# Sliding-window attention: the two halves of a unit's probabilities are added into one square before they are transposed

## The chip, the cores and the metric

The kernel runs on one core of a Trainium2 chip. The metric is the device time of one execution in microseconds (us). The whole network of four layers is one program; the change concerns two of the four layers.

## The reference, cut to what matters

The model is a stack of four layers over 16 learned tokens and 1024 input tokens of width 1024: attention, mLSTM, HGRN2, attention. The change lies in the attention layers (`i % 3 == 0`, that is layers 0 and 3). There a block of 128 queries sees its own block of 128 keys and the one before, within a window of 128:

```python
dist = (jnp.arange(BLOCK)[:, None] + BLOCK) - jnp.arange(2 * BLOCK)[None, :]
band = (dist >= 0) & (dist < A_WIN)          # BLOCK = A_WIN = 128
s = jnp.where(mask, einsum(q, kk) * A_HD ** -0.5, -jnp.inf)
m = jnp.maximum(s.max(axis=-1), sink)
e = jnp.exp(s - m[..., None])
p = e / (e.sum(axis=-1) + jnp.exp(sink - m))[..., None]
o = jnp.einsum('bnhgqk,bnkhd->bnqhgd', p, vv)
```

For query i of a block the band keeps key j (0 to 255, the block before first) where j > i and j <= i + 128. So of the keys j and j + 128 exactly one is inside the window of each query: where the left half of a row of `p` is not zero the right half is zero, and the reverse. This is what the change uses.

## The kernel before

Each layer projects its input on TensorE (PE) with float32 operands split into a high and a low part, so that each product is three matmuls (L231 for the tiles of weights, L281, L326 for the output projection). PE's order is written out: a list of steps, each with a cost in nanoseconds, in which two lists are merged in proportion to their costs by `weave`. The order on VectorE (DVE), ScalarE (ACT), GpSimd (POOL) and the DMA queue (SP) is set by a scheduler that follows data dependencies and priorities.

The attention itself is cut into units. A unit is one block `b` of queries (9 blocks of which block 0 has the 16 learned tokens), one `pair` of tiles of heads (4 pairs) and one half `hh` of those tiles; it handles two heads, index `u`. Layer 0 has 72 units and layer 3 has 64, since it leaves out block 0. The units of a pair run one after the other, with block as the outer and `hh` as the inner loop. While one pair is attended, PE also gets the projections for later pairs ("fill"), and these differ by pair: little of it beside pairs 0 and 3, more beside pairs 1 and 2. A unit has three steps, two units apart on PE: at the turn of unit k, PE gets V_step of unit k-4, T_step of unit k-2, S_step of unit k.

- **S_step** (L701): four matmuls make the scores `S` [128, 2, 256] in PSUM (L726, L727). A custom DVE operation (L734, one per head) adds the mask, scales, and leaves the scores and their row minimum in the SBUF tile `Sm`; ACT takes the exponential in place with the row's sum (L737, one per head); DVE takes the reciprocal (L739); POOL multiplies the 2 x 256 probabilities by it (L740). POOL also writes the sink's column of `Sm` ahead of that (L731). `Sm` has two buffers, so units k and k+2 share one.
- **T_step** (L743): PE transposes `Sm` in four pieces of 128 x 128 (two halves, two heads, L755) into one PSUM tile `pt`. ACT copies `pt` to `Ph`, the part of higher value (L757), and DVE subtracts it from `pt` to make `Pl` (L758).
- **V_step** (L760): four matmuls with `Ph` and `Pl` (L773) add up the output `po`, which ACT and DVE move to the rows `o` (L781, L782).

The mask tile `masks` is read by L734 at its columns 128 to 383; its entry is 0 inside the window and 1e30 outside, because L734 works with the sign reversed and takes a minimum.

Of the kernel before, what the change touches and what calls it, by code (L numbers as in the profile page):

```python
# [9 lines left out]
F32 = mybir.dt.float32  # L10
F32R = mybir.dt.float32r
AF = mybir.ActivationFunctionType
ALU = mybir.AluOpType
PSUM = bass.MemoryType.PSUM

P = 128
# [97 lines left out]
def hybrid_kernel(ctx: ExitStack, tc: tile.TileContext, ins, out, layers=(0, 1, 2, 3)):  # L114
    nc = tc.nc
    v, s, g, pe, sp = nc.vector, nc.scalar, nc.gpsimd, nc.tensor, nc.sync
# [11 lines left out]
    def nm(x):  # L128
        ctr[0] += 1
        return f"{x}{ctr[0]}"  # L130
# [16 lines left out]
    def psum(tag, bufs):  # L147
        return ps.tile([P, 512], F32, tag="p", name=nm(tag), bufs=8)
# [331 lines left out]
    def layer_a(i, j, first, last, fin, scale=None):  # L480
# [3 lines left out]

        def enter():
            R["mix"] = mix = new_mix()
            R["masks"] = masks = mix.tile([P, 384], F32, name=nm("masks"))
            sp.dma_start(masks, ins["a_masks"])
            R["cons"] = cons = mix.tile([P, 18], F32, name=nm("cons"))
            sp.dma_start(cons, ins["a_cols"][j])  # L490
            v.tensor_scalar(cons[:, 0:1], cons[:, 0:1], -0.125, None, op0=ALU.mult)
            v.tensor_scalar(cons[:, 2:18], cons[:, 2:18], -1.0, None, op0=ALU.mult)
# [205 lines left out]
        def mixers():  # L698


            def S_step(w):  # L701
                mix, cons = R["mix"], R["cons"]
                b, hh, n = w["b"], w["hh"], w["n"]
                kh, kl = R["k", w["pair"] // 2][hh]
                q0, nq = blk(b)
                qb = slice(q0 - chunks[n][0], q0 - chunks[n][0] + nq)
                kq = CHUNK_BLOCKS[n].index(b)
                if b == 0:
                    k0, kbs = 0, ((0, 0, 16),)
                elif b == 1:  # L710
                    k0, kbs = 0, ((0, 0, 16), (1, 16, 128))
                else:
                    k0, kbs = q0 - P, ((b - 1, 0, 128), (b, 128, 128))
                w["kbs"] = kbs
                nk = sum(z[2] for z in kbs)
                kw, mo = (nk if b == 0 else 256), {0: 128, 1: 112}.get(b, 0)
                kb = slice(k0, k0 + kw)
                S = psum("pm", 2).rearrange("p (u k) -> p u k", u=2)
                w["Sm"] = Sm = mix.tile([P, 2, 257], F32, tag="Sm", name=nm("Sm"), bufs=2)
                if b == 0:  # L720
                    g.memset(Sm[:, :, :NMETA], 0.0)
                st, den = small(2), small(2)
                sinks = []
                for u, t in enumerate(w["ts"]):
                    q = R["q", t, n][hh]
                    pe.matmul(S[:nq, u, :kw], q[:, qb], kh[:, kb], start=True, stop=False)  # L726
                    pe.matmul(S[:nq, u, :kw], q[:, qb], kl[:, kb], start=False, stop=True)  # L727
                    head = (2 * (t // 4) + hh) * 4 + t % 4
                    sinks.append(cons[:nq, 2 + head : 3 + head])
                    if u == 0:  # L730
                        g.tensor_copy(Sm[:nq, :, nk : nk + 1], cons[:nq, 2 + head : 4 + head].rearrange("p (u c) -> p u c", c=1))  # L731
                for u in range(2):
                    rq = R["rq", w["ts"][u], n][:nq, 2 * kq + hh : 2 * kq + hh + 1]
                    v.tensor_tensor_reduce(Sm[:nq, u, :nk], S[:nq, u, :nk], R["masks"][:nq, P + mo : P + mo + nk],  # L734
                                           rq, sinks[u], ALU.add, ALU.min, st[:nq, u : u + 1])
                for u in range(2):
                    s.activation(Sm[:nq, u, : nk + 1], Sm[:nq, u, : nk + 1], AF.Exp, scale=-1.0,  # L737
                                 bias=st[:nq, u : u + 1], accum_out=den[:nq, u : u + 1])
                v.reciprocal(den[:nq], den[:nq])  # L739
                g.tensor_tensor(Sm[:nq, :, :nk], Sm[:nq, :, :nk],  # L740
                                den[:nq].rearrange("p (u c) -> p u c", c=1).to_broadcast([nq, 2, nk]), op=ALU.mult)

            def T_step(w):  # L743
                b, kbs, Sm = w["b"], w["kbs"], w["Sm"]
                nq = blk(b)[1]
                kn = NMETA if b == 0 else P
                pt = psum("pt", 1).rearrange("p (k u q) -> p k u q", k=2, u=2)
                w["Ph"] = Ph = R["mix"].tile([P, 2, 2, P], F32R, tag="Ph", name=nm("Ph"), bufs=2)
                w["Pl"] = Pl = R["mix"].tile([P, 2, 2, P], F32R, tag="Pl", name=nm("Pl"), bufs=2)
                if b == 0:  # L750
                    for z in (Ph, Pl):
                        g.memset(z[:, 0, :, :NMETA].bitcast(F32), 0.0)
                for ki, (kb, ko, _) in enumerate(kbs):
                    for u in range(2):
                        pe.transpose(pt[:kn, ki, u, :], Sm[:, u, ko : ko + kn], ident)  # L755
# [800 lines left out]
def _layout(inp):  # L1556
# [1 line left out]
    meta, xx = np.asarray(inp["meta"]), np.asarray(inp["x"])[0]  # L1558
    f["xT"] = np.concatenate([meta, xx], axis=0).T.reshape(KT, P, T)
    f["ngain"] = np.asarray(inp["norm_gain"]).reshape(4, KT, P).transpose(2, 0, 1)  # L1560
    am = np.zeros((P, 384), np.float32)
    am[:64, :64] = 1.0
    am[64:, 64:128] = 1.0
    ii = np.arange(P)[:, None]
    jj = np.arange(256)[None]
    am[:, 128:] = np.where((jj > ii) & (jj <= ii + P), 0.0, -BIG)
    f["a_masks"] = am
    f["b_mask"] = np.where(ii <= np.arange(P)[None], 0.0, BIG).astype(np.float32)
# [76 lines left out]
```

## Time and profile before

| what | value |
|---|---|
| time of three runs, median (lowest to highest) | 2595.86 us (2591.49 to 2597.38) |
| the profiled execution: its time, its span | 2594.76 us, 2593.0 us |
| granted TensorE clock, mean | 0.997 |
| PE busy | 2547.2 us (98%) |
| DVE, ACT, POOL busy | 1949.5 us (75%), 1682.9 us (65%), 243.4 us (9%) |
| units of attention with `b > 1` | 56 in each of the two layers, 112 in all |

The share of an engine is its busy time over the span of all four layers; attention takes about the first 415 us and the stretch from about 2200 to 2530 us. A row of a group of instructions names the line of the kernel, the engine, the operation, what is written and read, the shapes and the count; then busy us and mean ns of one; then how long the engine was idle just before and what ended that. A row of the timeline begins with the start in us from the start of the span and the duration.

### The profile page before, as it was taken

The page shows a single profiled execution, that of the slowest core. Times are in us where ns is not written, and L with a number is a line of the kernel's source. Part 1 is how long each engine was busy: PE and PEld are TensorE (multiplying, and loading weights), DVE is VectorE, ACT ScalarE, POOL GpSimd, SP SyncE. Part 2 cuts the span into 40 slices and gives each one's busy share as a digit, 9 for nine tenths or more (in the row PEclk, how much of TensorE's full clock was granted, in tenths as well). Part 3 has the DMA queues.
Part 4 walks back from the last instruction along what each step waited for, and adds up shares of the span by engine and source line. Part 5 has one row for each costly group of instructions (what it writes and reads, how often), then busy time and mean ns, then how long its engine had stood idle before and what let it go on. Part 6 is the DMA issues. An engine that isn't in the chain of part 4 may idle for free.

```text
span 2593.0 us, 54342 instructions
## 1 busy us (share of the span) xinstructions
PE 2547.2 (98%) x20446; PEld 2487.2 (96%) x20446; DVE 1949.5 (75%) x5266; ACT 1682.9 (65%) x4403; POOL 243.4 (9%) x564
## 2 busy tenths in 40 slices
PE   8999999999999999999999999999999999999999
PEld 8899999999999999999999999999999999999999
DVE  7897898785657474747475688978878978887996
ACT  8766766576464555555555757877676857767772
POOL 0321231000000000000000000001000000321330
PEclk9999999999999999999999999999999999999999
DMA  5223212021111111111111111111111113212112
GB/s 157 62 66 95 57 43 70 29 67 54 46 50 49 51 41 58 42 50 45 53 42 50 58 35 34 35 35 35 34 42 34 35 51 93 64 43 82 56 42 78
DMA packets 86058, 140.21 MB, mean 54 GB/s; under 512 B 12425, under 2 KB 39186, under 8 KB 85794
## 3 DMA queue, kind: packets, MB, share of 16 engines
q1 hardware_dynamic: 85794, 136.73, 17.1%
q8 instruction: 161, 2.64, 0.4%
q14 instruction: 103, 0.84, 0.1%
HBM read 121.83 MB, written 4.27 MB: 49 GB/s over the span
## 4 chain that ended last, share of the span: by engine, by line
PE 62%; DVE 13%; ACT 8%; issue 2%; DMA 1%; SPq 0%; POOL 0%; DVEq 0%; ACTq 0%; POOLq 0%
PE pj L231 28%; PE pj L326 14%; PE pj L281 10%; DVE wl L196 1%; PE po L1019 1%; PE po L1021 1%; PE pa L1035 1%; ACT X L1269 1%; PE po L773 1%; DVE x L329 1%; PE pj L277 1%; ACT Sm L737 1%; PE pt L755 1%; DVE Sm L734 1%; DVE X L1267 1%
## 5 line engine op out<-in xcount | busy, mean ns | idle before, releaser
L231 PE MATMUL pj<-uh,wh 128*128 128x256 f32 (+2 forms) x2688 | 915.7, 341 | 7.7 <-ACT uh L401 7.2
L231 PE MATMUL pj<-ul,wh 128*128 128x256 f32 (+2 forms) x2688 | 864.3, 322 | 0.3
L231 PE MATMUL pj<-uh,wl 128*128 128x256 f32 (+2 forms) x2688 | 864.6, 322 | 0.0
L231 PEld LDWEIGHTS pj<-uh,wh 128*128 128x128 f32 x2688 | 508.5, 189 | 17.4 <-ACT uh L401 7.2
L231 PEld LDWEIGHTS pj<-ul,wh 128*128 128x128 f32 x2688 | 508.8, 189 | 6.4 <-DVE ul L196 0.8
L231 PEld LDWEIGHTS pj<-uh,wl 128*128 128x128 f32 x2688 | 507.9, 189 | 0.0
L196 DVE TENSOR_TENSOR wl<-wr,wh 128x512 fp32r<-128x512 f32 (+1 forms) x338 | 234.2, 703 | 55.0 <-ACT wh L195 52.1
L195 ACT CAST wh<-wr 128x512 fp32r<-128x512 f32 (+1 forms) x338 | 202.7, 613 | 97.6 <-PE pj L326 31.5
L326 PE MATMUL pj<-yh,wh 128*128 128x384 f32 (+2 forms) x768 | 253.6, 330 | 9.8 <-DVE x L329 8.3
L329 DVE TENSOR_TENSOR x<-x,pj 128x384 f32<-128x384 f32 (+2 forms) x480 | 233.8, 507 | 33.4 <-PE pj L326 32.1
L326 PE MATMUL pj<-yh,wl 128*128 128x384 f32 (+2 forms) x768 | 246.2, 321 | 0.0
L326 PE MATMUL pj<-yl,wh 128*128 128x384 f32 (+2 forms) x768 | 246.2, 321 | 0.0
L281 PE MATMUL pj<-wh,uh 128*128 128x256 f32 (+1 forms) x768 | 232.7, 303 | 0.0
L281 PE MATMUL pj<-wl,uh 128*128 128x256 f32 (+1 forms) x768 | 216.3, 282 | 0.0
L281 PE MATMUL pj<-wh,ul 128*128 128x256 f32 (+1 forms) x768 | 215.9, 281 | 0.0
L737 ACT ACTIVATE Sm<-Sm,s 128x257 f32<-128x257 f32 (+2 forms) x272 | 131.1, 483 | 88.6 <-DVE s L734 86.3
L740 POOL TENSOR_TENSOR Sm<-Sm,s 128x512 f32<-128x512 f32 (+2 forms) x136 | 139.3, 1024 | 406.5 <-DVE s L739 386.3
L458 ACT ACTIVATE t<-t 128x384 f32<-128x384 f32 (+2 forms) x240 | 118.0, 491 | 75.5 <-DVE t L457 74.6
L195 ACT CAST yh<-r 128x384 fp32r<-128x384 f32 (+2 forms) x120 | 57.0, 478 | 156.2 <-PE pj L326 139.4
L326 PEld LDWEIGHTS pj<-yh,wh 128*128 128x128 f32 x768 | 144.9, 189 | 14.0 <-DVE x L329 10.3
L457 DVE SCALAR_TENSOR_TENSOR t<-pj,t 128x400 f32<-128x400 f32 (+2 forms) x168 | 86.3, 513 | 81.5 <-ACT t L456 80.2
L281 PEld LDWEIGHTS pj<-wh,uh 128*128 128x128 f32 x768 | 144.7, 188 | 2.2
(303 smaller groups left out, 5447.1 us busy)
## 6 DMA issues: line engine op xcount, KB each, us to landing
wr<-in_b_win SPq DMA_DIRECT2D x124, 256.0 KB, 2.8
wr<-in_a_win SPq DMA_DIRECT2D x80, 256.0 KB, 2.8
wr<-in_c_win SPq DMA_DIRECT2D x64, 256.0 KB, 3.0
wr<-in_a_wout SPq DMA_DIRECT2D x32, 256.0 KB, 2.8
wr<-in_b_wout SPq DMA_DIRECT2D x32, 256.0 KB, 2.7
t<-t SPq DMA_DIRECT2D x100, 48.0 KB, 1.9
cs<-in_rope SPq DMA_DIRECT2D x11, 400.0 KB, 3.7
cs<-in_rope SPq DMA_DIRECT2D x11, 384.0 KB, 3.5
```

Of the source, the lines that this page charges most:

```text
L195: s.copy(h, src)
L196: v.tensor_tensor(l, src, h.bitcast(F32), op=ALU.subtract)
L231: pe.matmul(acc[:, :cn], a[:, k, :], b[:, k, c0 : c0 + cn], start=(k == 0 and i == 0), stop=(k == KT - 1 and i == 2))
L277: pe.matmul(acc[:48, :nc], um[0][:, k, :], m[:, kk, :], start=(k == 0 and m is wh), stop=(k == KT - 1 and m is wl))
L281: pe.matmul(acc[:cn, :nc], a[:, k, c0 : c0 + cn], m[:, kk, :], start=(k == 0 and j == 0), stop=(k == KT - 1 and j == 2))
L326: pe.matmul(acc[:, :cn], a[:, k, mc], b, start=(k == 0 and i == 0), stop=(k == 1 and i == 2))
L329: v.tensor_tensor(x[:, m, c0 : c0 + cn], x[:, m, c0 : c0 + cn], acc[:, :cn], op=ALU.add)
L457: v.scalar_tensor_tensor(a[:, :cn], z, 0.0, a[:, :cn], op0=ALU.min, op1=ALU.subtract)
L458: s.activation(a[:, :cn], a[:, :cn], AF.Exp)
L734: v.tensor_tensor_reduce(Sm[:nq, u, :nk], S[:nq, u, :nk], R["masks"][:nq, P + mo : P + mo + nk], rq, sinks[u], ALU.add, ALU.min, st[:nq, u ...
L737: s.activation(Sm[:nq, u, : nk + 1], Sm[:nq, u, : nk + 1], AF.Exp, scale=-1.0, bias=st[:nq, u : u + 1], accum_out=den[:nq, u : u + 1])
L740: g.tensor_tensor(Sm[:nq, :, :nk], Sm[:nq, :, :nk], den[:nq].rearrange("p (u c) -> p u c", c=1).to_broadcast([nq, 2, nk]), op=ALU.mult)
```

## The change

For the units with `b > 1`, POOL first adds the right half of `Sm` to the left (L742 of the new kernel), so that a square of 128 x 128 per head holds all 128 keys of each query's window. The multiplication by the reciprocal (L743) then covers 2 x 128 elements instead of 2 x 256, and PE makes two transpositions instead of four (L758). A DVE operation takes the minimum of each transposed square with a mask of 1e30 or 0, once for either half, and writes the 2 x 2 x 128 results back to the buffer of `Sm` (L762). ACT copies from there to `Ph` (L763), and the subtraction that makes `Pl` moves from DVE to POOL (L764). The mask is a window of one more column in `masks`, which grows from 384 to 385 columns. Blocks 0 and 1 are as before.

```diff
                 v.reciprocal(den[:nq], den[:nq])
+                if b > 1:
+                    nk = P
+                    g.tensor_tensor(Sm[:, :, :P], Sm[:, :, :P], Sm[:, :, P : 2 * P], op=ALU.add)
                 g.tensor_tensor(Sm[:nq, :, :nk], Sm[:nq, :, :nk],
                                 den[:nq].rearrange("p (u c) -> p u c", c=1).to_broadcast([nq, 2, nk]), op=ALU.mult)
...
-                pt = psum("pt", 1).rearrange("p (k u q) -> p k u q", k=2, u=2)
+                pt = psum("pt", 1)
...
+                if b > 1:
+                    for u in range(2):
+                        pe.transpose(pt[:, P * u : P * u + P], Sm[:, u, :P], ident)
+                    src = Sm.rearrange("p u k -> p (u k)")[:, :512].rearrange("p (k u q) -> p k u q", k=2, u=2)
+                    both = pt[:, : 2 * P].rearrange("p (k u q) -> p k u q", k=1, u=2)
+                    keep = R["masks"][:, P + 1 : 3 * P + 1].rearrange("p (k u q) -> p k u q", k=2, u=1)
+                    v.tensor_tensor(src, both.to_broadcast([P, 2, 2, P]), keep.to_broadcast([P, 2, 2, P]), op=ALU.min)
+                    s.copy(Ph, src)
+                    g.tensor_tensor(Pl, src, Ph.bitcast(F32), op=ALU.subtract)
+                    return
+                pt = pt.rearrange("p (k u q) -> p k u q", k=2, u=2)
...
-    jj = np.arange(256)[None]
+    jj = np.arange(257)[None]
```

On PE the order of the steps is the same before and after; only the run of four transpositions of a unit becomes a run of two. The queues of the other engines are laid anew by the scheduler. GpSimd's queue in pair 0 of layer 0, before, for units 11, 12 and 13 (`Sm_1359`, `Sm_1407`, `Sm_1454` are their tiles of probabilities, `cons` holds the sinks, `s` the reciprocal):

```order
L731 COPY Sm_1359<-cons_188 128x2
L740 TENSOR_TENSOR Sm_1303<-Sm_1303,s_1305 128x2x256
L731 COPY Sm_1407<-cons_188 128x2
L740 TENSOR_TENSOR Sm_1359<-Sm_1359,s_1361 128x2x256
L731 COPY Sm_1454<-cons_188 128x2
L740 TENSOR_TENSOR Sm_1407<-Sm_1407,s_1409 128x2x256
```

The same place after, where the tiles of the three units are `Sm_1360`, `Sm_1408` and `Sm_1455`, and `Pl_1401`, `Pl_1442` are the results of the subtraction for units 10 and 11:

```order
L742 TENSOR_TENSOR Sm_1360<-Sm_1360 128x2x128
L743 TENSOR_TENSOR Sm_1360<-Sm_1360,s_1362 128x2x128
L764 TENSOR_TENSOR Pl_1401<-Sm_1304,Ph_1400 128x512
L731 COPY Sm_1408<-cons_188 128x2
L742 TENSOR_TENSOR Sm_1408<-Sm_1408 128x2x128
L743 TENSOR_TENSOR Sm_1408<-Sm_1408,s_1410 128x2x128
L764 TENSOR_TENSOR Pl_1442<-Sm_1360,Ph_1441 128x512
L731 COPY Sm_1455<-cons_188 128x2
```

One multiplication per unit has become an addition, a multiplication and a subtraction, and the subtraction for a unit stands behind the multiplication of the next unit. Of the 112 units, 100 have this order; in 12 the subtraction stands ahead of that multiplication.

VectorE's queue at the same place, before (unit 12; `pm` are its scores):

```order
L734 ISA Sm_1407,s_1408<-pm_1406,masks_186,cons_188,rq_570 128x256
L734 ISA s_1408 128x1
L758 TENSOR_TENSOR Pl_1399<-pt_1397,Ph_1398 128x512
L734 ISA Sm_1407,s_1408<-pm_1406,masks_186,cons_188,rq_634 128x256
L734 ISA s_1408 128x1
L528 TENSOR_TENSOR qs_1475<-t_1239,qs_1475 64x400
L782 TENSOR_TENSOR r_977<-r_977,po_1323 64x256
L739 RECIPROCAL s_1409<-s_1409 128x2
```

And after, from unit 12's scores to those of unit 13:

```order
L734 ISA Sm_1408,s_1409<-pm_1407,masks_186,cons_188,rq_570 128x256
L734 ISA s_1409 128x1
L734 ISA Sm_1408,s_1409<-pm_1407,masks_186,cons_188,rq_634 128x256
L734 ISA s_1409 128x1
L762 TENSOR_TENSOR Sm_1360<-pt_1440,masks_186 128x512
L796 TENSOR_TENSOR r_977<-r_977,po_1325 64x256
L739 RECIPROCAL s_1410<-s_1410 128x2
L528 TENSOR_TENSOR qs_1477<-t_1241,qs_1477 64x400
L528 TENSOR_TENSOR qs_1480<-t_1241,qs_1480 64x400
L796 TENSOR_TENSOR r_978<-r_978,po_1325 64x256
L734 ISA Sm_1455,s_1456<-pm_1454,masks_186,cons_188,rq_570 128x256
```

The minimum for unit 11 (L762) stands behind the scores of unit 12 and ahead of its reciprocal, and the first operation on unit 13's scores writes into the buffer that unit 11 has had, so it waits for the subtraction `Pl_1442` on GpSimd.

More of the change, by code (lines that the diff above doesn't have):

```diff
@@ L486, in enter @@
             R["mix"] = mix = new_mix()
-            R["masks"] = masks = mix.tile([P, 384], F32, name=nm("masks"))
+            R["masks"] = masks = mix.tile([P, 385], F32, name=nm("masks"))
             sp.dma_start(masks, ins["a_masks"])
```

2 lines of the change are left out of this document (1 added, 1 removed).

## The prediction

> **What bounds the kernel now.** I read the page first: how busy the engines are, and the chain that ended last.
>
> ```profile
> PE 2547.2 (98%) x20446; PEld 2487.2 (96%) x20446; DVE 1949.5 (75%) x5266; ACT 1682.9 (65%) x4403; POOL 243.4 (9%) x564
> PE 62%; DVE 13%; ACT 8%; issue 2%; DMA 1%; SPq 0%; POOL 0%; DVEq 0%; ACTq 0%; POOLq 0%
> ```
>
> PE is busy nearly all the time and holds most of the chain. GpSimd is on it with 0%. So a transposition saved looks like time saved, and work on GpSimd looks free. Those are averages over four layers, so next I look at the attention alone: how far apart are the units? Each unit has four transpositions, so their first and last start in a stretch, and their count, give the period. First four stretches beside pairs 0 and 3, then two of pair 1, then two of pair 2:
>
> ```profile
> L755 PE MATMUL pt<-ident,Sm x48: 270/272/330, 82.3 to 121.5; 128*128 128x128 f32 x48
> L755 PE MATMUL pt<-ident,Sm x44: 270/272/328, 361.2 to 397.3; 128*128 128x128 f32 x44
> L755 PE MATMUL pt<-ident,Sm x48: 270/272/328, 2212.7 to 2251.0; 128*128 128x128 f32 x48
> L755 PE MATMUL pt<-ident,Sm x48: 270/272/275, 2476.0 to 2517.2; 128*128 128x128 f32 x48
> L755 PE MATMUL pt<-ident,Sm x48: 270/272/299, 155.5 to 217.3; 128*128 128x128 f32 x48
> L755 PE MATMUL pt<-ident,Sm x48: 270/272/273, 2277.8 to 2342.9; 128*128 128x128 f32 x48
> L755 PE MATMUL pt<-ident,Sm x56: 270/272/306, 279.4 to 341.6; 128*128 128x128 f32 x56
> L755 PE MATMUL pt<-ident,Sm x56: 270/272/300, 2399.1 to 2462.7; 128*128 128x128 f32 x56
> ```
>
> Less 0.3 us for the last unit's own four, the first four rows are 11, 10, 11 and 11 periods in 38.9, 35.8, 38.0 and 40.9 us: 43 periods of 3.57 us on average, the quick stretches. Pair 1 has 5.6 and 5.9 us, pair 2 has 4.8 and 4.9 us. So PE gives the other engines 3.57 us per unit at the least. What do they do with it? Two of the quick stretches by windows (busy us of PE, PEld, DVE, ACT, POOL), and who PE waited for in all of the program:
>
> ```profile
> 361.10:396.90 35.80, 34.99 (x248) 34.19 (x247) 32.65 (x87) 27.14 (x76) 13.96 (x20) 1.00 0.20 58
> 2212.70:2250.60 37.90, 37.90 (x286) 37.58 (x284) 32.79 (x96) 30.54 (x94) 14.98 (x23) 1.00 0.17 49
> PE pt L755 <- POOL Sm L740: 10.0, 9, 2.2
> PEld pt L755 <- POOL Sm L740: 12.9, 12, 2.5
> ```
>
> PE is full there, but VectorE is at 91% and 87%, GpSimd at 39%. And of the few waits that PE has in attention, the one that comes back is for GpSimd's multiplication (22.9 us in 21 times). Attention is close to a second bound, the way from scores to transposition.
>
> **The change: what PE saves.** The timeline shows the four transpositions of a unit as one piece, and the groups give the mean of one:
>
> ```profile
> 200.36 0.60 PE L755 MATMUL pt<-ident,Sm 128*128 128x128 f32 x4
> L755 PE MATMUL pt<-ident,Sm 128*128 128x128 f32 x512 | 77.4, 274 | 8.3 <-POOL Sm L740 7.8 <-DVE s L734 0.4
> ```
>
> 0.60 us less 0.274 for the last one to end is three spacings, 0.11 us each. Two fewer are 0.22 us per unit, 112 x 0.22 = 24.6 us, if PE waits for nothing new.
>
> **What the other engines get.** The rows that carry it:
>
> ```profile
> L740 POOL TENSOR_TENSOR Sm<-Sm,s 128x512 f32<-128x512 f32 x112 | 124.2, 1109 | 260.6 <-DVE s L739 242.5 <-DVE rq L603 5.1 <-PE pm L727 4.8
> L740 POOL TENSOR_TENSOR Sm<-Sm,s 128x288 f32<-128x288 f32 x16 | 11.1, 693 | 134.2 <-DVE s L739 132.1 <-PE pt L755 2.0
> L758 DVE TENSOR_TENSOR Pl<-pt,Ph 128x512 fp32r<-128x512 f32 x128 | 87.9, 687 | 12.9 <-ACT Ph L757 11.3
> L757 ACT CAST Ph<-pt 128x512 fp32r<-128x512 f32 x128 | 74.3, 581 | 13.7 <-PE pt L755 12.7
> 211.52 1.04 POOL L740 TENSOR_TENSOR Sm<-Sm,s 128x512 f32<-128x512 f32 x1 [3.33 <-DVE s L739]
> ```
>
> On VectorE a subtraction of 512 elements out of PSUM (0.69 us) gives way to a minimum of 512 elements out of PSUM: I take the same 0.69. On ScalarE the cast stays at about 0.58. Neither engine's load moves. GpSimd goes from one operation of 1.04 us to three. From 288 to 512 elements its mean grows by 1.86 ns per element, so 256 elements come to 0.63 us; the addition and the shorter multiplication make 1.27 together. The subtraction has 512 elements and two inputs, and no row shows it on GpSimd: its bounds are VectorE's 0.69 and GpSimd's own 1.11, and I take 1.04, since that is GpSimd's undisturbed rate for this size. GpSimd then has 2.3 us of work per unit instead of 1.04, which fits into 3.57.
>
> The Trainium skill, GPSIMD Engine Reference, section 4.1, speaks against such a move: elementwise work belongs on VectorE, as GpSimd is about twice as slow with two inputs. Here the rows say 1.04 against 0.69, 1.5 times; by the page's factor the subtraction would be an estimated 1.38 us, and the forecast below would rise to about 2655 us.
>
> **The wait that is added.** Load is not what decides, but order. GpSimd's new queue has, for nearly every unit: addition and multiplication for k+1, subtraction for k, then addition and multiplication for k+2. The subtraction for k is the last reader of the buffer that k and k+2 share, so VectorE's first operation on the scores of k+2 waits for it. That closes a ring of one unit's period: subtraction k, scores k+2, exponentials, reciprocal, multiplication k+2, subtraction k+1. Before, the buffer came free as soon as PE had transposed it, and there was no such ring. Its length can be read off a unit of a quick stretch, whose scores ran undisturbed:
>
> ```profile
> 393.44 0.53 DVE L734 CUSTOM_DVE_ANT_0 Sm<-pm,masks,cons 128x256 f32<-128x256 f32 x1
> 393.90 0.54 DVE L734 CUSTOM_DVE_ANT_0 Sm<-pm,masks,cons 128x256 f32<-128x256 f32 x1
> 394.07 0.51 ACT L737 ACTIVATE Sm<-Sm,s 128x257 f32<-128x257 f32 x1
> 394.58 0.50 ACT L737 ACTIVATE Sm<-Sm,s 128x257 f32<-128x257 f32 x1
> 394.98 0.18 ACT L737 ACTIVATION_READ_ACCUMULATOR Sm<-Sm,s 128x1 f32 x1
> 395.20 0.17 DVE L739 RECIPROCAL s<-s 128x2 f32<-128x2 f32 x1
> 395.28 0.67 DVE L196 TENSOR_TENSOR wl<-wr,wh 128x512 fp32r<-128x512 f32 x1
> 395.45 1.40 POOL L740 TENSOR_TENSOR Sm<-Sm,s 128x512 f32<-128x512 f32 x1 [1.47 <-DVE s L739]
> 395.87 1.41 DVE L475 TENSOR_TENSOR t<-t,t 128x400 f32<-128x400 f32 x1
> 397.80 0.56 DVE L476 TENSOR_TENSOR r<-r,t 128x400 f32<-128x400 f32 x1
> 103.04 0.53 DVE L734 CUSTOM_DVE_ANT_0 Sm<-pm,masks,cons 128x256 f32<-128x256 f32 x1
> 105.79 1.04 POOL L740 TENSOR_TENSOR Sm<-Sm,s 128x512 f32<-128x512 f32 x1
> ```
>
> From the first score operation to the start of the multiplication it is 395.45 - 393.44 = 2.01 us. The addition needs only the exponentials (done at 395.16), not the reciprocal, so it begins 0.25 us earlier, and addition plus multiplication end where the one long multiplication would have ended undisturbed, 2.01 + 1.04 = 3.05 us. Then the subtraction, 1.04, and a signal to VectorE, 0.08 as from the reciprocal's end (395.37) to the multiplication. The floor of the ring is 4.2 us, above the 3.57 us of the quick stretches: each transposition, which needs its multiplication, would come at the pace of the ring, and PE with its strict order idles.
>
> Two things lengthen it. Where other VectorE work stands between scores and reciprocal, the 2.01 are more: in the last two rows, from another quick stretch, 105.79 - 103.04 = 2.75. In the new queue the minimum for the unit before (0.69 us) and often one fill operation stand there. And the two engines get in each other's way: the multiplication at 395.45 took 1.40 instead of 1.04, since L196 was running, and L475, whose like at 397.80 took 0.56, took 1.41 and ended 0.43 us after the multiplication. With twice the GpSimd work there are more such meetings. The Trainium skill, SBUF — State Buffer, "Who interferes with whom", states the rule: a VectorE instruction with two SBUF inputs and a GpSimd one that reads SBUF exclude each other, and the second blocks. The trace agrees, 1.41 against 0.56 us; the new minimum reads PSUM and one SBUF tile, so by the rule it escapes.
>
> I take half of the 0.74 us (2.75 less 2.01) and half of a meeting's 0.36 us (1.40 less 1.04): 4.2 + 0.37 + 0.18, about 4.7 us. Ends: 4.2 with neither, 5.3 with both in full.
>
> **The sum.**
>
> - Quick stretches: 43 x (4.7 - 3.57) = +48.6 us.
> - Pair 1, 28 units: its period is above the ring, PE saves 28 x 0.22 = -6.2 us.
> - Pair 2, 28 units at 4.81: PE alone could do 4.59, the ring stops it at 4.7: 28 x 0.11 = -3.1 us.
> - The remaining 13 units of pairs 0 and 3, at the ends of their pairs, have longer periods: 13 x 0.22 = -2.9 us.
>
> Together +36.4 us. The profiled execution took 2594.76 us, 1.1 below the median of the runs, so I forecast 2631 us. With the floor of 4.2 it is 43 x 0.63 = +27.1, less 69 x 0.22 = 15.2: +11.9, 2607 us. With 5.3: +74.4, -6.2, +13.7 (pair 2 slowed by 0.49), -2.9: +79, 2674 us.
>
> Edits that I put at nothing: the mask's one column more, a few bytes in one transfer at the start of a layer; and `Pl`, which is ready later by up to a period and a subtraction, where V_step comes two whole periods after the transposition.
>
> **Rivals.**
>
> 1. PE stays the bound and the change does what the saved transpositions suggest: -24.6 us, 2570 us, faster. For it: PE at 98 to 100% in the quick stretches, and only 22.9 us of waits for GpSimd. It needs a ring below 3.57 - 0.22 = 3.35 us; even the undisturbed unit gives 4.2. It could be so if the subtraction ran ahead of the next multiplication far more often than the queue shows. 0.12.
> 2. Meetings decide: VectorE's fill is mostly of operations with two SBUF inputs, and both the multiplication and the subtraction meet one, with waits for the scores on top. The ring is then 5.3 + 0.36, about 5.6 us: 43 x 2.03 = +87.3, pair 2 +22.1, pair 1 and the rest -9.1: +100, 2695 us. Against it: VectorE idles while it waits, which clears its queue. 0.09.
> 3. The gains and losses cancel: a ring of 3.9 us gives 43 x 0.33 = +14.2 against -15.2, 2594 us. It needs a subtraction at VectorE's 0.69. 0.03.
>
> **How the numbers follow.** The forecast has the remaining 0.76. The range goes from the floor's 2607 less 5 for the spread of the runs to 2674 plus 6: 2602 to 2680. Taking 0.2% (5 us) as what a measurement of this kernel can tell from no change: faster 0.12 (rival 1), same 0.03 (rival 3), slower 0.85.
>
> **What would show it.** In the new profile the quick stretches should show transpositions 4.2 to 5.3 us apart, PE waiting at L758 for L743 by tens of us, and L734 on VectorE waiting for L764. Pair 1 should be 0.2 us per unit quicker. If PE's waits for GpSimd stay near 23 us, the ring is not there and rival 1 is right. If L743 and L764 are far above 0.63 and 1.04 us, it is rival 2.

## The result and the profile after

The changed kernel takes 2687.44 us (median of five runs, 2685.37 to 2690.01). The kernel before, on the same chip, takes 2597.38 (2591.49 to 2598.36). The ratio is 1.0351, 95% interval 1.0336 to 1.0366: slower by some 91 us. The forecast had the direction and the ring of waits; the size (+36, at most +85 by the range) was too small, and pairs 1 and 2 went the other way than it said.

The page of the changed kernel: busy time, and the chain that ended last (which here is followed back over less than a fifth of the span, so I use it for nothing).

```profile
PE 2568.7 (96%) x20222; PEld 2489.9 (93%) x20222; DVE 1990.7 (74%) x5266; ACT 1696.2 (63%) x4403; POOL 441.5 (16%) x788
PE 5%; DVE 4%; issue 3%; POOL 3%; ACT 2%; DMA 0%; SPq 0%; ACTq 0%; DVEq 0%; POOLq 0%
```

PE has 224 instructions fewer and is busy 21.5 us longer. VectorE is busy 41 us longer with the same number of instructions. GpSimd went from 243 to 441 us. Who waits, over the whole program (line, who is waited for: us, times, longest):

```profile
PE pt L758 <- POOL Sm L743: 53.6, 39, 3.6
PEld pt L758 <- POOL Sm L743: 65.5, 44, 3.9
DVE Sm L734 <- POOL Pl L764: 72.9, 66, 2.4
POOL Pl L764 <- ACT Ph L763: 87.0, 53, 32.1
```

Three signs that the prediction named are there: PE waits for the multiplication by tens of us, VectorE's score operation waits 66 times for the subtraction, a wait that did not exist before, and the period of the quick stretches is longer. A fourth, a quicker pair 1, is not. The period, by the same reading as in the prediction (first and last transposition of a stretch and their count, now two per unit). Four quick stretches, then two of pair 1, then two of pair 2:

```profile
L758 PE MATMUL pt<-ident,Sm x24: 270/298/421, 81.6 to 131.7; 128*128 128x128 f32 x24
L758 PE MATMUL pt<-ident,Sm x24: 270/273/474, 395.3 to 447.7; 128*128 128x128 f32 x24
L758 PE MATMUL pt<-ident,Sm x24: 270/273/476, 2256.7 to 2309.5; 128*128 128x128 f32 x24
L758 PE MATMUL pt<-ident,Sm x24: 270/273/475, 2558.4 to 2611.0; 128*128 128x128 f32 x24
L758 PE MATMUL pt<-ident,Sm x24: 270/272/301, 168.8 to 232.4; 128*128 128x128 f32 x24
L758 PE MATMUL pt<-ident,Sm x24: 270/272/330, 2336.4 to 2407.6; 128*128 128x128 f32 x24
L758 PE MATMUL pt<-ident,Sm x24: 270/273/333, 301.0 to 365.4; 128*128 128x128 f32 x24
L758 PE MATMUL pt<-ident,Sm x24: 270/273/329, 2468.5 to 2531.8; 128*128 128x128 f32 x24
```

Each row is eleven periods and one spacing of 0.1 us. The quick stretches have 4.5, 4.8, 4.8 and 4.8 us, 4.7 on average, the number of the forecast. But pair 1 has 5.8 and 6.5 us where it had 5.6 and 5.9, and pair 2 has 5.8 and 5.7 where it had 4.8 and 4.9. Both were expected to gain.

The stretches of pairs 1 and 2 whole, by windows from the first score matmul of a pair to that of the next (PE, PEld, DVE, ACT, POOL busy; clock). Pair 1 and 2 of layer 0, then of layer 3; the kernel before first, then after:

```profile
127.40:255.00 127.60, 125.20 (x839) 119.82 (x837) 105.54 (x271) 86.75 (x241) 24.85 (x45) 1.00 0.28 81
255.00:338.90 83.90, 81.89 (x580) 80.39 (x579) 74.80 (x205) 62.40 (x185) 21.80 (x41) 1.00 0.22 63
2256.80:2381.70 124.90, 122.59 (x833) 120.04 (x832) 99.57 (x243) 83.59 (x227) 21.59 (x33) 1.00 0.25 75
2381.70:2459.80 78.10, 76.72 (x541) 74.88 (x539) 68.09 (x174) 57.97 (x166) 21.63 (x31) 1.00 0.16 47
```
```profile
137.90:276.80 138.90, 127.54 (x810) 118.96 (x809) 111.35 (x279) 90.83 (x246) 51.86 (x74) 0.98 0.26 75
276.80:370.90 94.10, 84.86 (x554) 79.45 (x552) 78.05 (x204) 62.91 (x182) 47.21 (x69) 0.96 0.19 53
2315.60:2451.40 135.80, 123.74 (x805) 119.81 (x805) 109.78 (x251) 86.48 (x231) 48.56 (x64) 0.97 0.24 69
2451.40:2540.60 89.20, 78.56 (x513) 74.38 (x511) 71.98 (x173) 58.87 (x167) 46.73 (x60) 0.96 0.14 41
```

Together these stretches grew from 414.5 to 458.0 us, +43.5: PE's busy time by 8.3 and its idle time (length less busy) from 8.1 to 43.3. Pairs 0 and 3, measured the same way, grew by 52.4 us. So more than half of the slowdown lies where the forecast put it (it had 48.6 less 2.9 there), and the miss lies in pairs 1 and 2, where it had -9.3.

In pair 1 over half of the loss lies in one place. Read from score matmul to score matmul, its units together took 4.6 us more in layer 0 and 5.9 in layer 3. The end of the pair, where PE runs projections and starts no scores, took 42.3 us in both layers where it had taken 35.5 and 37.3: 11.8 of the pair's 22.3 us.

### The profile page after: what moved, and what is told of

It is laid out like the page before. It is cut to its first block, busy times and chain, and to the rows that moved or that the text cites. A ratio compares the mean times of both kernels' runs of the same rounds, so it can differ in the third digit from the quotient of the medians.

```text
span 2687.9 us, 54253 instructions
## 1 busy us (share of the span) xinstructions
PE 2568.7 (96%) x20222; PEld 2489.9 (93%) x20222; DVE 1990.7 (74%) x5266; ACT 1696.2 (63%) x4403; POOL 441.5 (16%) x788
## 5 line engine op out<-in xcount | busy, mean ns | idle before, releaser
L231 PEld LDWEIGHTS pj<-uh,wh 128*128 128x128 f32 x2688 | 514.2, 191 | 17.5 <-ACT uh L401 6.4
L196 DVE TENSOR_TENSOR wl<-wr,wh 128x512 fp32r<-128x512 f32 (+1 forms) x338 | 242.9, 729 | 55.2 <-ACT wh L195 51.7
L734 DVE CUSTOM_DVE_ANT_0 Sm<-pm,masks,cons 128x256 f32<-128x256 f32 (+2 forms) x272 | 130.6, 511 | 77.5 <-POOL Pl L764 72.9
L764 POOL TENSOR_TENSOR Pl<-Sm,Ph 128x512 fp32r<-128x512 f32 x112 | 158.2, 1412 | 125.9 <-ACT Ph L763 87.0
L326 PEld LDWEIGHTS pj<-yh,wh 128*128 128x128 f32 x768 | 146.5, 191 | 21.5 <-DVE x L329 7.9
L326 PEld LDWEIGHTS pj<-yl,wh 128*128 128x128 f32 x768 | 146.6, 191 | 5.3 <-DVE yl L196 5.0
```

The lines of the kernel that those rows point to most:

```text
L196: v.tensor_tensor(l, src, h.bitcast(F32), op=ALU.subtract)
L231: pe.matmul(acc[:, :cn], a[:, k, :], b[:, k, c0 : c0 + cn], start=(k == 0 and i == 0), stop=(k == KT - 1 and i == 2))
L326: pe.matmul(acc[:, :cn], a[:, k, mc], b, start=(k == 0 and i == 0), stop=(k == 1 and i == 2))
L764: g.tensor_tensor(Pl, src, Ph.bitcast(F32), op=ALU.subtract)
```

## The experiments

All times are medians of four executions (five of the changed kernel), and each ratio is against the kernel before on the same chip (2591 to 2594 us, 2597 for the changed kernel). The runs were on several chips, so differences between them are given by the ratios. This table shows where each kernel lost time against the kernel before: the length of the pairs, from score matmul to score matmul in the traces (pair 3 up to its last unit), both layers together, from one profiled execution each. The row for the changed kernel without rotation stands against its own base.

| kernel | time, us | ratio (95%) | pairs 0, 3 | pairs 1, 2 |
|---|---|---|---|---|
| changed | 2687.44 | 1.0351 (1.0336–1.0366) | +52.4 | +43.4 |
| 1 own buffer | 2603.14 | 1.0042 (1.0026–1.0059) | +2.9 | +6.8 |
| 2 two transpositions alone | 2580.37 | 0.9955 (0.9940–0.9970) | -6.0 | -3.8 |
| 3 subtraction without the cast | 2668.34 | 1.0299 (1.0284–1.0314) | +40.2 | +33.3 |
| 4 subtraction on VectorE | 2650.68 | 1.0226 (1.0210–1.0241) | +32.7 | +24.0 |
| 5 half a subtraction | 2633.83 | 1.0159 (1.0144–1.0174) | +26.9 | +13.2 |
| 6 hold in the kernel before | 2669.51 | 1.0299 (1.0282–1.0317) | +42.0 | +34.7 |
| 7 reciprocal put back | 2699.86 | 1.0413 (1.0398–1.0429) | +62.3 | +43.0 |
| 8, 9 no rotation, before and after | 2576.72, 2652.95 | 0.9941 (0.9925–0.9956), 1.0231 (1.0211–1.0250) | +49.7 | +28.8 |
| 10 spare work, all pairs | 2721.43 | 1.0496 (1.0477–1.0515) | +61.4 | +59.4 |
| 11 spare work, pairs 0 and 3 | 2716.86 | 1.0481 (1.0464–1.0497) | +66.9 | +46.0 |

**1. Is it the shared buffer?** The result of the minimum goes to `Pl` instead of back to `Sm`; all operations stay.

```diff
-                    src = Sm.rearrange("p u k -> p (u k)")[:, :512].rearrange("p (k u q) -> p k u q", k=2, u=2)
+                    src = Pl.bitcast(F32)
...
-                    v.tensor_tensor(src, both.to_broadcast([P, 2, 2, P]), keep.to_broadcast([P, 2, 2, P]), op=ALU.min)
+                    v.tensor_tensor(Pl, both.to_broadcast([P, 2, 2, P]), keep.to_broadcast([P, 2, 2, P]), op=ALU.min)
```

> The minimum is written into the buffer of Pl instead of back into Sm, and the cast and the subtraction read it there; the same operations of the same sizes otherwise (the value is rounded on that write, so the low part comes out as zero). Sm is then free as soon as PE has transposed it. Theory (a ring through the shared buffer: subtraction, scores two units on, exponentials, addition, multiplication, next subtraction): the ring is gone, PE saves most of 24.6 us less some 10 to 30 us for GpSimd's longer way to the transposition: 2572 to 2610 us, no wait of VectorE's L734 for the subtraction. Rival (the load: three GpSimd operations instead of one, meeting VectorE's operations with two SBUF inputs): the same operations meet as before, the time stays above 2650 us.

2603.14 us, inside the theory's range. The waits of this kernel at the transpositions, and its subtraction (shortest, median, longest in ns):

```profile
PEld pt L758 <- POOL Sm L743: 17.2, 22, 2.5
PE pt L758 <- POOL Sm L743: 11.9, 13, 2.2
L764 POOL TENSOR_TENSOR Pl<-Pl,Ph x112: 1265/1293/1737, 85.8 to 2539.6; 128x512 fp32r<-128x512 f32 x112
```

The subtraction is as long as ever and still stands between the multiplications on GpSimd. Only nobody's scores wait for it: VectorE's wait at L734 for L764 is gone from the list, PE's wait for the multiplication falls to 11.9 us, near the 10.0 of the kernel before, and some 80 us of the slowdown are gone, in all four pairs. The ring through the buffer is shown.

**2. What are two transpositions worth?** The kernel before with the transpositions of the left halves only; nothing is added on GpSimd or VectorE.

```diff
-                for ki, (kb, ko, _) in enumerate(kbs):
+                for ki, (kb, ko, _) in enumerate(kbs[:1] if b > 1 else kbs):
...
+                if b > 1:
+                    src = pt[:, 0:1].to_broadcast([P, 2, 2, P])
+                    s.copy(Ph, src)
+                    v.tensor_tensor(Pl, src, Ph.bitcast(F32), op=ALU.subtract)
+                    return
```

> The kernel before with only the two transpositions of the left halves; the cast and the subtraction read the one square for both halves, so the right halves of the probabilities are left out of the result. Nothing else changes. Theory (PE is the bound in the kernel before and 0.11 us is the price of a transposition): 24.6 us less, 2566 to 2576 us. Rival (the way from scores to transposition was the bound already, so PE only waits more): above 2585 us.

2580.37 us, between the two numbers, 11.7 us faster than the kernel before by the ratio. From the start of the matmul before the run to the end of its last matmul it is 0.77 us with four and 0.56 with two (medians), so the price of 0.22 us per unit was right. But less than half of the 24.6 arrives at the end: pairs 1 and 2 of layer 0 gave nothing back (+3.7 and -0.9 us), those of layer 3 gave 5.1 and 1.5. Of the +3.7, 3.1 lie in the end of pair 1, where the granted clock was at a half for 6.8 us in this run and at full speed before. So the saving with nothing added is worth 0.45%. Experiments 1 and 2 together cost the change's other half: the same saving with GpSimd's addition and subtraction beside it, and no ring, is 23 us worse. That takes in both GpSimd's load and the longer way from the exponentials to the transposition.

**3. Which part of the ring, the cast?** The subtraction takes the identity in place of `Ph`, so it needs no cast.

```diff
-                    g.tensor_tensor(Pl, src, Ph.bitcast(F32), op=ALU.subtract)
+                    g.tensor_tensor(Pl, src, ident.rearrange("p (k u q) -> p k u q", k=1, u=1).to_broadcast([P, 2, 2, P]), op=ALU.subtract)
```

> The changed kernel, but GpSimd subtracts the identity instead of Ph, with the same number of elements, so the subtraction no longer waits for ScalarE's cast (Pl holds another value). Theory (in pairs 1 and 2 the ring runs over reciprocal, minimum and cast, which stand later in their queues than the multiplication, about 1.0 us per unit there): pairs 1 and 2 come back by 25 to 50 us, pairs 0 and 3 by less than 15 us, 2630 to 2660 us. Rival (pairs 1 and 2 lose by the same ring as pairs 0 and 3, or by VectorE's load, and the cast lies beside it): 2675 to 2690 us.

2668.34 us, 13 us less than the changed kernel by the ratios. The two profiled executions are 22 us apart, 12 in pairs 0 and 3 and 10 in pairs 1 and 2. Neither number: the cast is a link, not the one that decides. In pair 1 the subtraction then began 0.85 us after the next multiplication's end on average, for now it waited for the minimum, where it had been 1.01.

**4. Move the subtraction back to VectorE**, with the minimum still in the shared buffer.

```diff
-                    g.tensor_tensor(Pl, src, Ph.bitcast(F32), op=ALU.subtract)
+                    v.tensor_tensor(Pl, src, Ph.bitcast(F32), op=ALU.subtract)
```

> The changed kernel with the subtraction on VectorE. GpSimd keeps addition and multiplication. The buffer is still held until the subtraction. Theory (the ring's length decides): the subtraction takes 0.69 instead of 1.41 us and no longer stands behind GpSimd's multiplication, but VectorE, at 87 to 93% in attention, gets 0.69 us more per unit (77 us in all): 2630 to 2670 us, VectorE over 95% busy in pairs 1 and 2. Rival (meetings of the two engines decide): with GpSimd at 1.5 us per unit instead of 2.9 the time falls to 2620 us or less.

2650.68 us, as the theory had it, though VectorE was busy 86 to 93% of the stretches of pairs 1 and 2 and not over 95. Its group on VectorE:

```profile
L764 DVE TENSOR_TENSOR Pl<-Sm,Ph 128x512 fp32r<-128x512 f32 x112 | 85.0, 759 | 6.9 <-ACT Ph L763 6.3
```

0.76 us instead of 1.41: the ring has a shorter link, but VectorE, which is itself a link, has 85 us more to do.

**5. Halve one link.** The subtraction covers one half only, 256 elements, and V_step takes `Ph` in place of the missing half of `Pl`.

```diff
-                    g.tensor_tensor(Pl, src, Ph.bitcast(F32), op=ALU.subtract)
+                    g.tensor_tensor(Pl[:, 0], src[:, 0], Ph[:, 0].bitcast(F32), op=ALU.subtract)
```

> The changed kernel with the subtraction on GpSimd for one of the two halves only (256 elements instead of 512; for the other half the products with Pl take Ph once more, so its low part is left out). By the addition of the same size the subtraction should take 0.74 instead of 1.41 us. Theory (the ring sets the period in all four pairs): every unit is quicker by 0.5 to 0.67 us until PE is reached, pairs 0 and 3 by about 25 us, pairs 1 and 2 by about 30 us, 2620 to 2645 us. Rival (VectorE's load sets the period in pairs 1 and 2): only pairs 0 and 3 come back, 2655 to 2670 us.

2633.83 us, as the theory had it. The subtraction in this kernel:

```profile
L764 POOL TENSOR_TENSOR Pl<-Sm,Ph 128x256 fp32r<-128x256 f32 x112 | 96.9, 865 | 128.4 <-ACT Ph L763 124.1 <-PE pm L727 1.9 <-PE pt L758 1.1
```

1412 - 865 = 0.55 us less per unit, 61 us of GpSimd's time (its mean in the changed kernel is shown further down), and 50 us of the program's time by the ratios. The pairs' lengths fell by 25 us (pairs 0 and 3) and 30 us (pairs 1 and 2). So a microsecond of the subtraction is nearly a microsecond of time, in pairs 1 and 2 too. The forecast had taken pair 1 for bound by PE and pair 2 for nearly so.

**6. Put the ring into the kernel before.** An operation of GpSimd after the cast reads `Ph` and writes `Sm`, so the buffer is held as in the change; no addition, no minimum, four transpositions as before, and nobody reads what it writes.

```diff
+                if b > 1:
+                    z = Sm.rearrange("p u k -> p (u k)")[:, :512]
+                    g.tensor_tensor(z, z, Ph.rearrange("p k u q -> p (k u q)").bitcast(F32), op=ALU.subtract)
```

> The kernel before, with its four transpositions and the subtraction on VectorE, and with one more GpSimd operation per unit behind the cast, of 512 elements, which reads Sm and Ph and writes Sm (nobody reads it). It puts the ring into the kernel before: GpSimd operation, scores two units on, exponentials, multiplication, next GpSimd operation, 1.31 + 0.04 + 2.0 + 1.04 = 4.4 us at least, 4.4 to 4.9 with queues. Theory (the ring): pairs 0 and 3 slower by 40 to 55 us, pairs 1 and 2 by 0 to 15 us, since the cast there needs no minimum, 2632 to 2662 us. Rival (meetings of GpSimd and VectorE): the same operation costs 10 to 25 us spread over all pairs, 2600 to 2616 us.

2669.51 us, above the theory's range. Its groups:

```profile
L761 POOL TENSOR_TENSOR Sm<-Sm,Ph 128x512 f32<-128x512 f32 x112 | 153.0, 1366 | 127.6 <-ACT Ph L757 125.8 <-ACT rq L606 1.5
L734 DVE CUSTOM_DVE_ANT_0 Sm<-pm,masks,cons 128x256 f32<-128x256 f32 x224 | 113.8, 541 | 46.2 <-POOL Sm L761 43.6 <-PE po L776 1.0 <-PE pj L326 0.7
```

One more GpSimd operation that holds the buffer makes 77 us of the change's 91, its own load included. It loses 42.0 us in pairs 0 and 3, as expected, and 34.7 in pairs 1 and 2, over twice as much as expected.

**7. Is it the late minimum?** On VectorE the minimum often stood behind the next unit's scores. Here the reciprocal, addition and multiplication of a unit are issued behind the T_step of the unit before.

```diff
-                v.reciprocal(den[:nq], den[:nq])
...
+                def norm(nk=nk):
+                    v.reciprocal(den[:nq], den[:nq])
...
+                w["norm"] = norm
```

> The changed kernel with reciprocal, addition and multiplication of a unit written behind the transposition step of the unit before; the operations are the same, and only queues move. Minima that stand behind the next unit's reciprocal on VectorE: in pairs 0, 1, 2 and 3 there were 4, 27, 20 and 7 of 28 each, now 0, 25, 9 and 2. Theory (in pairs 1 and 2 the ring runs over a minimum that stands behind the reciprocal): pair 2 is quicker by 5 to 12 us in both layers together, pairs 0 and 3 by up to 6, pair 1 stays within 4, 2670 to 2682 us. Rival (the place of the minimum does not matter): within 4 us of the changed kernel's 2687 us, no pair moved by more than 4 us.

2699.86 us: slower than the changed kernel, and pairs 1 and 2 lost 43.0 us as before. That story fell, and so did the rival, by which no pair would move: pairs 0 and 3 lost another 10 us.

**8 and 9. Is it VectorE's load?** In both kernels three VectorE operations of the fill are left out (the rotation of queries and keys).

```diff
-                    v.tensor_tensor(dst, dst, cos_sin[:, 0, :cn], op=ALU.mult)
-                    v.tensor_tensor(rot, rot, cos_sin[:, 1, :cn], op=ALU.mult)
-                    v.tensor_tensor(dst, dst, rot, op=ALU.add)
```

> The kernel before, with the three VectorE operations per chunk that turn the queries and keys (L625 to L627 of the changed kernel) left out, so queries and keys enter the scores unturned. They take some 19 us of VectorE's time in pair 1 of layer 0 and 11 in pair 2, about a tenth of those stretches. This run is the base for the next one. Expected for itself: 2570 to 2591 us, since VectorE is at about 90% in pairs 1 and 2 and PE idles there 4 to 5% in layer 0.

> The changed kernel with the same three operations left out. It is compared with the same kernel before without them, pair by pair. Theory (in pairs 1 and 2 the loss comes through VectorE: it is nearly full there, stands at the head of its queue for GpSimd's subtraction, and its fill for PE comes late): with a tenth of VectorE's load gone the loss of pairs 1 and 2 over both layers falls from 43 us to under 22, and this kernel is 60 to 75 us above its base. Rival (the ring's own links, scores to subtraction, are all that sets the pace in pairs 1 and 2, whatever VectorE has to do beside them): the loss there stays at 36 us or more, and this kernel is 85 to 100 us above its base. Pairs 0 and 3 have nearly none of these operations and should keep their 52 us by either.

2576.72 and 2652.95 us: 76 us apart where it was 91. The loss of pairs 1 and 2 fell from 43 to 28.8 us; the bounds were 22 and 36, so neither number. In these pairs VectorE was busy 314 us instead of 371, 15% less, and a third of the loss went with that. Over half of what came back lies at the end of pair 1, which now grew by 3.9 us and not by 11.8. Pairs 0 and 3 kept their loss (49.7).

**10 and 11. Is it PE's clock?** In the changed kernel the clock is at a half for 80 us of the eight pairs, 7 in the kernel before. Extra transpositions, which nobody reads, fill PE's idle time.

```diff
                 if b > 1:
+                    for z in range(4):
+                        pe.transpose(pt[:, (2 + z % 2) * P : (3 + z % 2) * P], ident, ident)
                     for u in range(2):
```

In run 11 the count is `8 if w["pair"] in (0, 3) else 0`.

> The changed kernel; ahead of the two transpositions of each unit with b > 1, PE gets four more that turn the identity into the unused half of pt (nobody reads them). They add PE work of 0.11 us each, 0.44 us per unit, 49 us in all, and stand just where PE waits for L743. Why: in the changed kernel TensorE's granted clock is at a half for 80 us of the attention, in pieces of 3.4 and 6.8 us, where the kernel before has 7 us. Theory: the clock is halved because PE idles while it waits for the ring, and this is the part of the loss that the ring alone does not give (at most half of 73 us, 37 us). Then PE work that fills the idling restores the clock to 0.995 or more, and the time falls by 10 to 30 us, to 2657 to 2677. Rival: the halved clock lies beside the waits and costs nothing, PE is the bound in pairs 1 and 2 and pays for the extra work there: 56 x 0.44 = 25 us, 2690 to 2712 us.

> As the run before, but eight extra transpositions per unit (0.88 us) and only in pairs 0 and 3, where PE idles about 1 us per unit; pairs 1 and 2 are as in the changed kernel. Theory (halved clock costs): half-clock time in pairs 0 and 3 falls from 53 us to under 15, these pairs lose 35 to 48 us instead of 52, and pairs 1 and 2 stay at 43 us with their own 27 us of half clock: 2670 to 2685 us. Rival (the halved clock costs nothing): pairs 0 and 3 keep 52 us or lose more, since eight transpositions nearly fill the idle time: 2687 to 2715 us.

2721.43 and 2716.86 us. The time at half clock falls to 20 and 34 us (in run 11, in pairs 0 and 3, from 53 to 14), and both kernels are slower than the changed one, by 38 and 34 us for 49 us of work each. Run 10 is above even the rival's 2712; run 11 is inside the rival's range at its upper end. So the clock can be restored without getting the time back. What the half clock alone costs stays open, for these runs add work and restore the clock at once: PE's busy time in the pairs of run 10 rose by 27 us and not by 49. PE's own stretching is at most half of the 73 us more that the changed kernel spends at half clock. The five executions of the changed kernel, 2690.0 us at a mean clock of 0.983 to 2685.4 at 0.990, hint at a smaller price.

These two runs show something else. The extra work was put ahead of the transpositions at which PE waits, in a kernel where PE idles some 0.8 us per unit, and it did not fill that time: in the pairs of run 10 PE idles 94 us where it had idled 96, and the pairs took 25 us more (17 in run 11; most of what is left came after the last units' scores). PE is a link of the ring too, and the next section says how.

## Why the prediction was right and wrong

**The ring, right.** Named with its links and its place, and shown by runs 1 and 6: the buffer held until the subtraction makes most of the slowdown. That 4.7 us in the quick stretches was taken and also measured is luck, as the next paragraph shows.

**The sizes of its links, wrong, and they cancelled.** The groups of the changed kernel (busy us, mean ns | idle before), and ahead of them the subtraction with its shortest, median and longest duration:

```profile
L764 POOL TENSOR_TENSOR Pl<-Sm,Ph x112: 1261/1306/1737, 84.5 to 2624.7; 128x512 fp32r<-128x512 f32 x112
...
L764 POOL TENSOR_TENSOR Pl<-Sm,Ph 128x512 fp32r<-128x512 f32 x112 | 158.2, 1412 | 125.9 <-ACT Ph L763 87.0 <-PE pj L231 34.1 <-PE pa L598 2.2
L742 POOL TENSOR_TENSOR Sm<-Sm 128x256 f32<-128x256 f32 x112 | 87.6, 782 | 195.1 <-ACT Sm L737 195.1
L743 POOL TENSOR_TENSOR Sm<-Sm,s 128x256 f32<-128x256 f32 x112 | 81.6, 729 | 12.6 <-DVE s L739 3.5 <-PE po L787 0.8 <-PE pj L231 0.6
L762 DVE TENSOR_TENSOR Sm<-pt,masks 128x512 f32<-128x512 f32 x112 | 76.6, 684 | 13.0 <-PE pt L758 11.8
L763 ACT CAST Ph<-Sm 128x512 fp32r<-128x512 f32 x112 | 69.1, 617 | 44.6 <-DVE Sm L762 43.2 <-DVE s L739 0.7
```

The minimum (0.684) is as taken. The subtraction is 1.41 us on average, 1.31 in the median, where 1.04 was taken and 1.11 was the upper bound; addition and multiplication are 1.51 where 1.27 was taken. So the bound from the multiplication was too low. Even the shortest subtraction took 1.26 us, so this is the operation's own price and not one of meetings with VectorE, as rival 2 had it. The likely reason, which no run took apart, is that the multiplication's second operand is one value per row and head, repeated, while the subtraction reads two full squares. The Trainium skill, GPSIMD Engine Reference, section 4.1, says about twice VectorE's time with two inputs, and here the rows agree: 1.31 against 0.69 is 1.9. The 2655 us that the prediction worked out from that rule would have been the better forecast, 32 us short instead of 56. The GpSimd operations together are 0.61 us longer than taken, and yet the quick stretches have the period that was forecast, since the subtraction in pairs 0 and 3 begins on average 0.45 us before the end of the multiplication that the forecast had ahead of it: in 10 of 48 units well before it, in most others as it ends. These pairs lost 52.4 us where 45.7 were forecast.

**Pairs 1 and 2, wrong.** The step that failed is "its period is above the ring, PE saves 28 x 0.22", and likewise the 4.7 us as a ceiling in pair 2. Two things were wrong in it. The ring is longer than 4.7 us. From the start of a subtraction to the end of the multiplication two units on, matched row by row in the changed kernel, it is 5.4 us in pairs 0 and 3, 5.2 in pair 1 and 5.3 in pair 2, with GpSimd's operations as long as above; in pair 2 this alone is over the 4.8 us that its units had. And the ring does not close there. The next subtraction also needs its own minimum and cast, which the prediction's ring leaves out. In pairs 0 and 3 they are done in time, but in pair 1 the subtraction begins on average 1.1 us after that multiplication's end and in pair 2 0.4 us. A turn then takes 6.3 and 5.6 us (the last units of each pair left out), above the periods of both pairs before. One turn in pair 2 of the changed kernel, from its timeline (start, duration):

```profile
317.42 1.29 POOL L764 TENSOR_TENSOR Pl<-Sm,Ph 128x512 fp32r<-128x512 f32 x1
317.47 1.79 DVE L196 TENSOR_TENSOR wl<-wr,wh 128x512 fp32r<-128x512 f32 x1
319.29 0.54 DVE L734 CUSTOM_DVE_ANT_0 Sm<-pm,masks,cons 128x256 f32<-128x256 f32 x1
320.97 0.42 DVE L796 TENSOR_TENSOR r<-r,po 64x256 f32<-64x256 f32 x1 [0.32 <-ACT r L795]
321.64 0.74 POOL L742 TENSOR_TENSOR Sm<-Sm 128x256 f32<-128x256 f32 x1 [2.34 <-ACT Sm L737]
321.68 0.67 DVE L762 TENSOR_TENSOR Sm<-pt,masks 128x512 f32<-128x512 f32 x1
322.38 0.62 ACT L763 CAST Ph<-Sm 128x512 fp32r<-128x512 f32 x1 [0.42 <-DVE Sm L762]
322.46 0.61 POOL L743 TENSOR_TENSOR Sm<-Sm,s 128x256 f32<-128x256 f32 x1
323.08 1.28 POOL L764 TENSOR_TENSOR Pl<-Sm,Ph 128x512 fp32r<-128x512 f32 x1
324.39 0.55 DVE L734 CUSTOM_DVE_ANT_0 Sm<-pm,masks,cons 128x256 f32<-128x256 f32 x1 [1.40 <-POOL Pl L764]
```

From subtraction to subtraction it is 5.66 us. The subtraction ends at 318.71, but VectorE is in a fill operation (L196), which met it and took 1.79 us, and the scores begin at 319.29, 0.58 late. From scores to addition it is 2.35. At the end VectorE stands 1.40 us at the head of its queue for the next subtraction and does no fill. And on the other side, the minimum and the cast come late: from the multiplication's end to the minimum of the same unit it is 2.3 us on average in the stretches of pairs 0 and 3, 5.7 in pair 1 and 4.5 in pair 2. In pair 1 about half of this passes before PE's written order reaches the transposition, and the rest before VectorE's queue reaches the minimum. In pair 2 nearly all of it is VectorE's queue, where the next unit's scores, which wait for the subtraction before, stand ahead of the minimum in all units. In pair 1 the subtraction waits for the cast in 19 of 20 units, 1.0 us past the multiplication it is queued behind.

In pair 2 PE waits at the transposition for the multiplication (5.1 and 6.0 us in the two layers, of 9.2 and 10.6 us of idle time). In pair 1 PE itself hardly waits for the ring. The waits of PE and of VectorE in pair 1 of layer 0, changed kernel:

```profile
PE pa L615 <- ACT t L576: 4.0, 1, 4.0
PE pj L326 <- DVE s L734: 2.4, 3, 1.5
PE pa L598 <- ACT t L576: 1.0, 2, 0.6
PE pt L758 <- POOL Sm L743: 0.7, 1, 0.7
DVE Sm L734 <- POOL Pl L764: 9.1, 8, 2.1
```

Over that stretch PE's waits are 11.4 us, where they were 2.3 before, and only 1.6 of them are at lines of the attention: the rest are projections whose operands come late. VectorE stood 9.1 us for the subtraction, in a stretch where it had been busy 83% of the time before (105.54 of 127.60) and where every unit has fill to do. That the one delays the other is argued from the trace. The end of pair 1, where no scores start, speaks for it: VectorE is busy there for 28.6 and 29.4 us in the two layers, where it was 23.4 and 23.8, with 127 operations where it had 108, so it does work there that it did earlier before. PE, at half clock for 10 us of these stretches, is busy 5.0 us longer in the two together, and idle for the rest of the 11.8. Runs 8 and 9 bear it out in part: with the rotation gone, a third of the loss of pairs 1 and 2 goes. Runs 5 and 10 show that the loss also answers to GpSimd's link and to PE: take 0.55 us from the link and these pairs get 30 us back, give PE 0.44 us more per unit and they lose another 16. How the remaining 28.8 us divide between them was not settled.

**What PE saves, half wrong.** 0.22 us per unit is right, but 24.6 us took all of it to be on the path: run 2 gave 11.7. One reading of the profile before was off, though no term of the sum hangs on it: the 22.9 us of waits for GpSimd's multiplication add PE and its weight load, which stood idle through the same stretches. Counted once they are 12.9 us, in 12 stretches.

**The sum as it came out**, by the ratios of the runs: saved transpositions -11.7 us (run 2), more GpSimd work beside VectorE +22.6 (run 1 against run 2), the ring +80 (changed kernel against run 1): +91. The three add up by construction, as each is the step from one run to the next; the shares are what was measured. Rivals 1 and 3 needed a ring below 3.4 and of 3.9 us, and it is longer. Rival 2, with 2695 us, had the size, and with +22 it had pair 2 (+21 measured). But it put +87 into the quick stretches and took 9 off pair 1 and the ends of the pairs; the trace has a period of 4.7 us in the quick stretches and not 5.6, and pair 1 lost 22.

## What to carry to other kernels

Before an operation is moved to a queue with idle time, ask what its input buffer holds up: here the operation took 1.4 us on an engine that was 9% busy, and cost some 80 us because scores two units on waited for its buffer. When the length of such a ring is added up, take in all that the releasing operation waits for: here its own minimum and cast came too late in the pairs with more work beside them, and stretches whose period had been above the ring as added up were slowed as well. A saving on an engine that looks full need not all arrive (11.7 of 24.6 us here), so a run with the saving alone is worth having first.

## What the runs showed of the hardware

The granted clock fell after shorter idling than I had expected. Three windows of the changed kernel, one after the other:

```profile
119.10:122.50 3.40, 3.36 (x29) 3.15 (x28) 2.90 (x8) 0.94 (x2) 3.10 (x4) 1.00 0.06 14
122.50:125.90 3.40, 1.23 (x12) 1.03 (x10) 3.40 (x10) 2.97 (x12) 2.96 (x5) 1.00 0.01 2
126.20:132.40 6.20, 6.20 (x31) 6.20 (x31) 5.21 (x12) 3.53 (x10) 2.69 (x4) 0.50 0.24 63
```

PE idles 2.17 of 3.40 us at full clock, and then runs at 0.50 for 6.2 us, busy all the time. The Trainium skill, TensorE: Matmul & The Clock Gate, "Why this matters for your kernels", warns of idle gaps above some 3 us. Here the clock fell after 2.17 us, in one piece, and of the 18 times that it fell in the attention of this kernel, 14 had no idle piece of PE above 3 us at or just before them. The mean clock of the changed kernel is 0.983 against 0.997.

On GpSimd the multiplication by one repeated value per row and head was cheaper than an operation with two full inputs: by the means of the groups 1.11 us against 1.41 for 512 elements (multiplication of the kernel before, subtraction of the changed one), 0.73 against 0.78 for 256 (multiplication and addition of the changed one). The shortest of each, which leave meetings out, are 1.03 against 1.26 and 0.60 against 0.72. The operations differ too, so the repeated input is the likely reason and not shown. It is not repetition of any kind: run 3's subtraction of the identity, which is read as the same 128 columns four times over, took at least 1.27 us.
